# A two-block network on one core: half of twelve experts' last projection moved behind the experts, beside the first products of the next layer

## The chip, the cores and the metric

The kernel runs on 1 core of one Trainium2 chip. The metric is device time in microseconds. Its engines are called as in the profile: PE (TensorE's matmuls), PEld (its weight loads), DVE (VectorE), ACT (ScalarE), POOL (GpSimd) and SP (the queue that issues nearly all loads).

## The reference, cut to what matters

256 tokens of width 1024 pass through a first block (a mixer and 16 experts), a normalisation, and two layers of a second block. Everything is float32.

```python
# first block, after the mixer
h = rmsnorm(x, g_ffn[l])
aff = jax.nn.softmax((h @ w_router[l]).astype(f32), axis=-1)
vals, idx = lax.top_k(jnp.swapaxes(aff, 1, 2), cap)          # cap = 32 tokens an expert
xe = h[bidx, idx]
gt = jnp.einsum('becd,edf->becf', xe, w_gate[l])              # 1024 -> 2048
up = jnp.einsum('becd,edf->becf', xe, w_up[l])
ye = jnp.einsum('becf,efd->becd', jax.nn.silu(gt) * up, w_down[l])   # 2048 -> 1024
ye = ye * vals[..., None].astype(ye.dtype)
x = x + jnp.zeros_like(x).at[bidx, idx].add(ye.astype(dt))
return rmsnorm(x, g_final)
# second block, for l in 0, 1
x = x + 0.5 * swiglu(rms_norm(x, norm_ffn1[l]), ffn1_wi[l], ffn1_wo[l])   # wi: 1024 -> 2 * 2816
h = rms_norm(x, norm_mix[l]); p = h @ w_in[l]
...                                                            # recurrent mixer, chunk attention, pooling of p_c
x = x + jnp.concatenate([y_a, y_b, y_c], axis=-1) @ w_out[l]
x = x + memory_cross_attention(...)
x = x + 0.5 * swiglu(rms_norm(x, norm_ffn2[l]), ffn2_wi[l], ffn2_wo[l])
```

## The kernel before

The 256 tokens lie as two tiles of 128 (`t` = 0, 1) in `s.x`. The kernel is written once through, fully unrolled, and a scheduler turns the order of the text into an order for each engine; each engine, and the load queue SP, then works through its own list in order. A load waits there until its slot is free.

**The expert stage** (`moe`). For each of the 16 experts `e`, 16 slices of w_gate and w_up and 8 slices of w_down, 1 MiB each, are loaded in the order of their use by `wload` (lines 930 and 934). A slice is used by four products of 32 stationary columns (the expert's 32 tokens, or a quarter of the hidden channels), which stand beside each other in PE (lines 1020 and 1050; each is recorded as two matmuls, so a slice has eight). After the 16 slices a Silu, a product and four transposes give `ht`, the hidden activations with channels on partitions. The 8 slices of w_down give 512 output channels for each `b` of 0 and 1, four slices (`t`) for each. The result `ye` is scattered back to the tokens by a product with `sc`, a transposed one-hot matrix with the router's weights (line 1062), and added to `s.x` (line 1063). Tokens are fetched for the experts by the products in `gather` (line 1006): expert 0's own first, those of experts 1 to 15 behind all its products with w_down.

Where a slice lands is fixed by a list of 18 places and two spare ones that are used once. After the first 20 slices, the 18 take turns:

```python
SPARE = ["X", "K1"]
RING2 = ["hTh", "hTl", "L0", "L1", "decay", "U", "z", "hA", "R", *["ring"] * 4, "xa", *["spl"] * 3, "sd"]
```

Places are buffers that the mixer before no longer needs; "ring" is the ring of four 8-KiB buffers through which the other layers load all their weights, and "spl" are the three pairs of buffers for split weights. X and K1 later hold the tokens of experts 4 to 15.

**The feed-forward layers** (`ffn`). `turn` transposes `s.x` to `s.hT` (channels on partitions, eight blocks `k` of 128 channels, each as a high part `hTh` and a low part `hTl`; lines 370 to 374). The factor of the normalisation is not in `hT`; it is applied to the products, since it is one number per token. A weight piece of 1 MiB (512 input channels by 512 outputs) is loaded to the ring, and `wsplit` splits each half of it into a high part `wh` (ACT, line 307) and a low part `wl` (DVE, line 308). `lin_A_steps` multiplies: for each half piece 12 matmuls of 512 columns (three terms, two blocks, two token tiles; line 468). Two pieces make a group with all 1024 input channels; a group for the gate and one for the up projection are followed by `ev_gate`, `ev_up` and `finish` (lines 1091, 1095, and 1079 to 1083: eight transposes and a split of the hidden activations). Five such pairs and one group of a gate and up half make 22 pieces. In the first layer (`first=True`) two normalisations follow on each other, `g_final` between them, so a chain of squares, sums and powers on DVE, ACT and POOL (lines 1101 to 1111) has to end before the first group is evaluated; it is placed behind the first two half pieces. The output product `out(b)` adds to `s.x` (line 1129); `lead` puts the first half of the next layer's `turn` inside `out(1)`.

**Banks.** Products accumulate in a pool of six PSUM banks (`acc`); a group holds two, a half of w_down one, a scatter one. Transposes have two banks of their own.

Of the kernel before, what the change touches and what calls it, by code (L numbers as in the profile page):

```python
# [236 lines left out]
RING2 = ["hTh", "hTl", "L0", "L1", "decay", "U", "z", "hA", "R", *["ring"] * 4, "xa", *["spl"] * 3, "sd"]  # L237
NF = 3
# [4 lines left out]
class Net:  # L243
    def __init__(s, ctx, tc, A):
# [8 lines left out]
        s.t2 = pool("t2", 5)  # L253
        s.acc = pool("acc", 6, space=PSUM)
# [17 lines left out]
    def slot(s, i, name, shape, dt=F32, tag=None):  # L272
        return s.sl.tile(shape, dt, name=name, tag=tag or f"s{i}")
# [104 lines left out]
    def turn(s, g):  # L378

        s.hT = [s.late.tile([P, KT, T], F32R, name=n, tag=n) for n in ("hTh", "hTl")]  # L380
        for b in range(2):
            s.to_T(s.x, g, *s.hT, kps=(2 * b, 2 * b + 1))
            yield
# [29 lines left out]
    def pieces(s, ap):  # L413

        w = None if ap is None else s.wload(ap)
        for c in range(2):
            yield s.piece() if ap is None else s.wsplit(w[:, 1024 * c:1024 * c + 1024])

# [29 lines left out]
    def lin_A_steps(s, aps, xT, kts, evac, cols=512, in_turn=False):  # L448
# [12 lines left out]
        for p in halves():  # L461
# [3 lines left out]
            for ts, part in ([((t,), terms) for t in range(2)] if last else [((0, 1), [u]) for u in terms]):  # L465
                for w, x, i, kk in part:
                    for t in ts:
                        s.nc.tensor.matmul(pss[t], x[:, n + kk, t * P:t * P + P], w[:, kk, :],  # L468
# [9 lines left out]
    def lin_A(s, aps, xT, kts, evac, cols=512):  # L478
        run(s.lin_A_steps(aps, xT, kts, evac, cols))


    def first(s):
        with s.tc.tile_pool(name="phmix", bufs=1) as s.sl:
# [433 lines left out]
    def moe(s):  # L917
        nc, A = s.nc, s.A
        E, C = 16, 32
        loads = itertools.count()  # L920
        V, VS = s.V1

        def wload(ap):


            i, n = next(loads), len(RING2)
            where = RING2[i] if i < n else SPARE[i - n] if i < n + 2 else RING2[(i - n - 2) % n]
# [84 lines left out]
        gather(0, (0, 1), 0, 1)  # L1012
        for e in range(E):
# [16 lines left out]
            pp = s.trb([P, T])  # L1030
            for t in range(2):
                rep = s.tmp([P, 4, C])
                nc.gpsimd.tensor_copy(rep, wt[:, t, e, :].unsqueeze(1).to_broadcast([P, 4, C]))  # L1033
                nc.tensor.transpose(pp[:, t * P:(t + 1) * P], rep.rearrange("p j c -> p (j c)"), s.ident)
            sc = s.tmp([P, T])
            nc.scalar.copy(sc, pp)
# [6 lines left out]
            ht = s.tmp([P, 4, P])  # L1043
            nc.vector.tensor_copy(ht, ph)
            py = [s.bank([P, 512]), s.bank([P, 512])]
            for b in range(2):
                for t in range(4):
# [823 lines left out]
```

## Time and profile before

| | |
|---|---|
| time, median of 3 runs | 2604.05 us (2599.95 to 2615.35) |
| the profiled execution | 2604.3 us, with a span of 2602.2 us |
| PE busy | 2258.5 us (87% of the span) |
| DVE busy | 1155.5 us (44%) |
| ACT busy | 842.0 us (32%) |
| chain that ended last | PE 56%, DMA 32%, DVE 8% |
| HBM read | 661.92 MB, 255 GB/s over the span |

The page divides the span into stages that look different: the mixer until about 360 us, the experts until about 1285 us, the second block behind them. Shares of the span are means over all of these. "Waits" and "chain" name what released an instruction; a window gives busy time in a stretch, in the order PE, PEld, DVE, ACT, POOL, with the number of instructions in brackets.

### The profile page before, as it was taken

Reading aid. Unit: us, or ns where it says so; the run is one execution under the profiler, and the core shown is the slowest. Engines: PE = TensorE matmul, PEld = TensorE weight load, DVE = VectorE, ACT = ScalarE, POOL = GpSimd, SP = SyncE. Lnnn points to the kernel's source line nnn. Section 1 sums busy time; section 2 is a strip of 40 time slices with the busy share of each in tenths; the row PEclk is TensorE's granted clock in tenths of the full one; section 3 lists DMA queues with packets and bytes.
Section 4 is the critical chain, followed back from the end, with each engine's and each line's share of the span. In section 5 each row is a group of like instructions: output and inputs, shape, how many; then the busy total and the mean of one; then the engine's idle time right before and its main releaser. Section 6 shows DMA issues by size and latency. Waiting matters only on the chain.

```text
span 2602.2 us, 33476 instructions
## 1 busy us (share of the span) xinstructions
PE 2258.5 (87%) x13705; PEld 1504.9 (58%) x13705; DVE 1155.5 (44%) x1699; ACT 842.0 (32%) x1297; POOL 226.9 (9%) x252
## 2 busy tenths in 40 slices
PE   7999888766666777666799999999999999999999
PEld 6988864111111111111288887788888888778887
DVE  6886843000000000000265586555555558665554
ACT  5653320000000000000244545355444445545543
POOL 3321300000000000000000141100000005110000
PEclk9999989878778777788899999999999999999999
DMA  5344589999999999999955524245555543424553
GB/s 200 130 146 140 235 316 407 420 426 425 426 425 426 425 426 425 426 426 426 387 207 175 180 95 160 83 163 192 179 191 181 182 175 112 144 86 166 185 179 129
DMA packets 104633, 665.14 MB, mean 256 GB/s; under 512 B 11808, under 2 KB 12192, under 8 KB 34848
## 3 DMA queue, kind: packets, MB, share of 16 engines
q1 hardware_dynamic: 103328, 660.12, 64.9%
q8 instruction: 107, 1.75, 0.3%
q10 hardware_dynamic: 1008, 1.84, 0.2%
q0 software_dynamic: 144, 1.05, 0.1%
q14 instruction: 46, 0.38, 0.0%
HBM read 661.92 MB, written 1.05 MB: 255 GB/s over the span
## 4 chain that ended last, share of the span: by engine, by line
PE 56%; DMA 32%; DVE 8%; ACT 2%; issue 1%; POOL 1%; SPq 0%; DVEq 0%; ACTq 0%; POOLq 0%
PE lA L468 32%; DMA wc<-in_w_down_dram 12%; DMA wc<-in_w_up_dram 10%; DMA wc<-in_w_gate_dram 9%; PE acc L430 7%; PE lA L1679 4%; DVE wl L308 1%; PE acc L1020 1%; PE acc L1006 1%; PE trb L1079 1%; PE acc L1050 1%; DMA wc<-in_ffn_wi_dram 1%; PE acc L313 1%; ACT wh L307 1%; PE acc L1441 1%
## 5 line engine op out<-in xcount | busy, mean ns | idle before, releaser
L308 DVE TENSOR_TENSOR wl<-wc,wh 128x1024 fp32r<-128x1024 f32 (+1 forms) x447 | 548.2, 1230 | 381.1 <-ACT wh L307 370.8
L307 ACT CAST wh<-wc 128x1024 fp32r<-128x1024 f32 (+1 forms) x454 | 471.9, 1042 | 551.3 <-PE lA L468 398.2
L1020 PE MATMUL acc<-wc,xe 128*32 128x512 f32 x2048 | 376.4, 786 | 174.2 <-DMA wc<-in_w_up_dram 92.8
L1020 PEld LDWEIGHTS acc<-wc,xe 128*32 128x32 f32 x2048 | 53.2, 121 | 482.3 <-DMA wc<-in_w_up_dram 220.6
L1039 DVE TENSOR_TENSOR tmp<-tmp,acc 128x512 f32<-128x512 f32 x16 | 11.0, 686 | 522.5 <-PE acc L1020 522.5
L468 PE MATMUL lA<-wh,hTl 128*128 128x512 f32 (+1 forms) x864 | 236.4, 390 | 0.0
L468 PE MATMUL lA<-wh,hTh 128*128 128x512 f32 (+1 forms) x864 | 230.0, 387 | 3.3 <-ACT hTh L373 3.3
L468 PE MATMUL lA<-wl,hTh 128*128 128x512 f32 (+1 forms) x864 | 228.0, 385 | 3.0 <-DVE wl L308 3.0
L1050 PE MATMUL acc<-wc,tmp 128*32 128x512 f32 x1024 | 170.4, 738 | 63.9 <-DMA wc<-in_w_down_dram 50.2
L468 PEld LDWEIGHTS lA<-wl,hTh 128*128 128x128 f32 x864 | 162.1, 189 | 34.4 <-DVE wl L308 4.1
L468 PEld LDWEIGHTS lA<-wh,hTh 128*128 128x128 f32 x864 | 160.9, 188 | 35.4 <-ACT hTh L373 5.1
L468 PEld LDWEIGHTS lA<-wh,hTl 128*128 128x128 f32 x864 | 159.0, 189 | 26.5
L1038 ACT ACTIVATE tmp<-acc 128x512 f32<-128x512 f32 x16 | 9.6, 597 | 508.8 <-PE acc L1020 508.8
L1063 DVE TENSOR_TENSOR x<-x,acc 128x512 f32<-128x512 f32 x64 | 44.0, 687 | 255.0 <-PE acc L1062 255.0
L1050 PEld LDWEIGHTS acc<-wc,tmp 128*32 128x32 f32 x1024 | 29.6, 123 | 187.9 <-DMA wc<-in_w_down_dram 104.2
L1059 ACT COPY tmp<-acc 128x512 f32<-128x512 f32 x32 | 18.7, 585 | 317.5 <-PE acc L1050 317.5
L468 PE MATMUL lA<-wl,hidh 128*128 128x512 f32 x352 | 96.1, 391 | 0.0
L468 PE MATMUL lA<-wh,hidh 128*128 128x512 f32 x352 | 94.4, 390 | 0.0
L468 PE MATMUL lA<-wh,hidl 128*128 128x512 f32 x352 | 94.1, 389 | 0.0
L430 PE MATMUL acc<-hTh,wl 128*128 128x256 f32 x544 | 81.3, 291 | 10.7 <-DVE wl L308 10.4
L430 PE MATMUL acc<-hTh,wh 128*128 128x256 f32 x544 | 85.9, 297 | 1.5 <-ACT wh L307 1.0
L1033 POOL COPY tmp<-ohwt 128x128 f32<-128x128 f32 x32 | 9.3, 293 | 847.4 <-PE trb L1042 646.0
(447 smaller groups left out, 3060.8 us busy)
## 6 DMA issues: line engine op xcount, KB each, us to landing
wc<-in_w_up_dram SPq DMA_DIRECT2D x117, 1024.0 KB, 18.4
wc<-in_w_gate_dram SPq DMA_DIRECT2D x102, 1024.0 KB, 18.5
wc<-in_w_down_dram SPq DMA_DIRECT2D x102, 1024.0 KB, 17.2
wc<-in_ffn_wi_dram SPq DMA_DIRECT2D x88, 1024.0 KB, 4.7
wc<-in_ffn_wo_dram SPq DMA_DIRECT2D x40, 1024.0 KB, 4.7
wc<-in_w_in_dram SPq DMA_DIRECT2D x39, 1024.0 KB, 4.7
wc<-in_w_gate_dram SPq DMA_DIRECT2D x52, 512.0 KB, 13.5
wc<-in_w_down_dram SPq DMA_DIRECT2D x52, 512.0 KB, 15.9
```

The costliest lines, as they stand in the source:

```text
L307: s.nc.scalar.copy(h[:, :n], w)
L308: (eng or s.nc.vector).tensor_tensor(l[:, :n], w, h[:, :n].bitcast(F32), op=OP.subtract)
L313: mm(out, a[0], b[0], start=start, stop=False)
L430: s.nc.tensor.matmul(ps[:, c, :], w[:, k, :], x[:, k, :], start=i + k == 0, stop=i == len(terms) - 1 and k == KT - 1)
L468: s.nc.tensor.matmul(pss[t], x[:, n + kk, t * P:t * P + P], w[:, kk, :], start=n + kk + i == 0, stop=i == 2 and n + kk == kts - 1)
L1006: nc.tensor.matmul(ps[:, i, :], s.x[:, t, k * P:(k + 1) * P], oh[:, t, 4 * g + lo:4 * g + hi].rearrange("p e c -> p (e c)"), start=t == 0, ...
L1020: nc.tensor.matmul(ps[32 * j:32 * j + 32, :], xe[e // 4, k // 4][:, k % 4, es], c(j), start=k == 0, stop=k == KT - 1)
L1050: nc.tensor.matmul(py[b][32 * j:32 * j + 32, :], ht[:, t, 32 * j:32 * j + 32], c(j), start=t == 0, stop=t == 3)
L1063: nc.vector.tensor_tensor(s.x[:, t, cs], s.x[:, t, cs], ps, op=OP.add)
L1079: nc.tensor.transpose(ps[:, j, t * P:(t + 1) * P], hs[t][:, (a + j) * P:(a + j + 1) * P], s.ident)
L1441: nc.tensor.matmul(ps[sl, it, :], lhs[sl, it, :], rhs[sl, it, :], start=True, stop=True, tile_position=(32 * gi, 32 * gi))
L1679: s.nc.tensor.matmul(pss[t], x[:, n + kk, t * P:t * P + P], w_[:, kk, :], start=n + kk + i == 0, stop=i == 2 and n + kk == KT - 1)
```

## The change

Experts 0 to 3 keep their order. For the last 12 experts (`LATE`) the main loop does only the first half of w_down (`b = 0`) and keeps `ht` in three places that leave the rotation from the second pass on (`KEPT`; 15 places stay). Behind expert 15, `turn` transposes channels 0 to 511, which are final then. A second loop does the second halves (`b = 1`) of the 12 experts; between its slices, from the sixth on, every second slice is followed by one step (half a piece) of `ffn_part`, which multiplies the first layer's 11 weight pieces for input channels 0 to 511 and copies the sums to six places (`PART`). In that loop slices rotate over six places (`EARLY_RING`), four of them the ring, which the pieces use as well. `ffn` then multiplies only channels 512 to 1023 in that layer (`products`) and adds the kept sums on DVE (`total`). Expert 0's gathers are placed between its second-half slices. `in_turn=b == 1` lets, in the last half piece of `out(1)`, all of token tile 0's matmuls come before tile 1's, with tile 0's sum evaluated between them, in all feed-forward layers and in the cross attention. `split_ahead` splits the pooling product's weights (`w_in[5]`) before the exponentials of the mixer instead of at the product. The places hTh and hTl, and those of `PART`, move to pools of their own.

```diff
 RING2 = [...]
+EARLY_RING = ["ring", "ring", "X", "ring", "ring", "K1"]
+LATE = 12
+KEPT = ["z", "R", "sd"]
+PART = ["L0", "L1", "decay", "U", "hA", "xa"]
...
     def moe(s):
...
-        loads = itertools.count()
+        rota = [[w for w in RING2 if w not in KEPT]]
+
+        def turns():
+            yield from RING2 + SPARE
+            while True:
+                now = rota[0]
+                for w in now:
+                    yield w
+                    if rota[0] is not now:
+                        break
+        places = turns()
...
-            i, n = next(loads), len(RING2)
-            where = RING2[i] if i < n else SPARE[i - n] if i < n + 2 else RING2[(i - n - 2) % n]
+            where = next(places)
...
+        def down(e, b, ht, sc):
+
+            py = s.bank([P, 512])
+            for t in range(4):
+                c = wload(A["w_down"][e, t, b])
+                for j in range(4):
+                    nc.tensor.matmul(py[32 * j:32 * j + 32, :], ht[:, t, 32 * j:32 * j + 32], c(j),
+                                     start=t == 0, stop=t == 3)
+                yield
+            cs = slice(512 * b, 512 * b + 512)
+            ye = s.tmp([P, 512])
+            nc.scalar.copy(ye, py)
+            for t in range(2):
+                ps = s.bank([P, 512])
+                nc.tensor.matmul(ps, sc[:, t * P:(t + 1) * P], ye, start=True, stop=True)
+                nc.vector.tensor_tensor(s.x[:, t, cs], s.x[:, t, cs], ps, op=OP.add)
+            yield
...
             if e == 0:
-                for g in range(4):
-                    for kk in (0, 4):
-                        gather(g, range(kk, kk + 4), int(g == 0), 4)
...
+                both = [down(e, b, ht, sc) for b in range(2)]
+                for j in range(8):
+                    next(both[j // 4])
+                    if j == 3:
+                        for kk in (0, 4):
+                            gather(0, range(kk, kk + 4), 1, 4)
+                    elif j > 3:
+                        for g, kk in others[2 * (j - 4):2 * (j - 4) + 2]:
+                            gather(g, range(kk, kk + 4), 0, 4)
+                for steps in both:
+                    run(steps)
+            else:
+                for b in range(2 if i < 0 else 1):
+                    run(down(e, b, ht, sc))
+
+
+        rota[0] = EARLY_RING
+        turn = s.turn(lambda k: s.gfg[:, k:k + 1])
+        next(turn)
+        parts = s.ffn_part()
+        n = 0
+        for e in kept:
+            steps = down(e, 1, kept[e], scale(e))
+            for _ in range(4):
+                next(steps)
+                n += 1
+                if n > 4 and n % 2 == 0 and n < 4 * LATE:
+                    next(parts, None)
+            run(steps)
+        run(parts)
+        run(turn)
+
+
+    def ffn_part(s):
+
+        wi = s.A["ffn1_wi"][0]
+        s.parts = {}
+        for i in range(6):
...
+            for g in range(2 if i < 5 else 1):
+                yield from s.lin_A_steps([wi[4 * i + 2 * g]], s.hT, 4,
+                                         lambda t, ps: s.nc.scalar.copy(s.parts[i][:, g, t, :], ps))
...
+            def products(c, evac):
+                if first:
+                    return s.lin_A_steps([wi[c + 1]], hT, 4, evac, k0=4)
+                return s.lin_A_steps([wi[c], wi[c + 1]], hT, 8, evac)
...
+                def total(j, t, ps, to=None):
+                    if not first:
+                        return ps
+                    to = s.tmp([P, 512]) if to is None else to
+                    nc.vector.tensor_tensor(to, ps, s.parts[i][:, j, t, :], op=OP.add)
+                    return to
...
-                    nc.scalar.activation(g[t], ps, AF.Silu, scale=r[:, t:t + 1])
+                    nc.scalar.activation(g[t], total(0, t, ps, g[t]), AF.Silu, scale=r[:, t:t + 1])
...
                     hs[t] = g[t]
+                    ps = total(1, t, ps)
...
-                return s.lin_A_steps([wo[5 * b + i] for i in range(5)] + [wt[b]], hid, 22, evac)
+                return s.lin_A_steps([wo[5 * b + i] for i in range(5)] + [wt[b]], hid, 22, evac, in_turn=b == 1)
...
+        w5 = s.split_ahead(w_in[5])
         nc.scalar.activation(flat(e1), flat(cl), AF.Exp)
...
-        s.lin_T(w_in[5], hT, lambda ps: vec.tensor_tensor(u, ps, rsb2, op=OP.mult))
+        s.lin_T(w5, hT, lambda ps: vec.tensor_tensor(u, ps, rsb2, op=OP.mult))
...
-        run(s.turn(lambda k: s.gfg[:, k:k + 1]))
```

## Rows read from the trace of the kernel before

**Rows 1.** The first line of the profile page

```profile
span 2602.2 us, 33476 instructions
```

**Rows 2.** Windows: us, busy us of each engine, granted clock, DMA, GB/s

```profile
452.00:1262.00 810.00, 563.62 (x2836) 100.59 (x2832) 56.39 (x82) 28.32 (x56) 7.93 (x27) 0.79 1.01 425
...
1298.00:1417.00 119.00, 119.00 (x545) 98.37 (x546) 70.19 (x79) 58.04 (x71) 2.53 (x3) 1.00 0.55 194
```

**Rows 3.** DMA issues: instruction and count, KB of each, median us to landing

```profile
wc<-in_w_down_dram SPq DMA_DIRECT2D x102, 1024.0 KB, 17.2
wc<-in_ffn_wi_dram SPq DMA_DIRECT2D x88, 1024.0 KB, 4.7
```

**Rows 4.** Timeline of the expert stage: start us, us, engine, line, operation, idle before

```profile
430.94 11.37 PE L1020 MATMUL acc<-wc,xe 128*32 128x512 f32 x104
...
442.23 0.44 PE L1034 MATMUL trb<-ident,tmp 128*128 128x128 f32 x2
...
1190.75 1.93 PE L1020 MATMUL acc<-wc,xe 128*32 128x512 f32 x8 [1.35 <-DMA wc<-in_w_gate_dram]
...
1275.51 1.98 PE L1062 MATMUL acc<-tmp 128*128 128x512 f32 x4
```

**Rows 5.** Chain of waits in the first feed-forward layer: start us, us, what

```profile
1312.80 0.22 PE trb L1079 x2
...
1314.14 21.33 PE lA L468 x94
1335.47 0.22 PE trb L1079 x2
```

**Rows 6.** Timeline at the end of the expert stage

```profile
1281.80 1.06 PE L1050 MATMUL acc<-wc,tmp 128*32 128x512 f32 x8 [1.15 <-DMA wc<-in_w_down_dram]
1282.93 0.58 ACT L1059 COPY tmp<-acc 128x512 f32<-128x512 f32 x1 [9.16 <-PE acc L1050]
...
1283.57 1.98 PE L1062 MATMUL acc<-tmp 128*128 128x512 f32 x4 [0.71 <-ACT tmp L1059]
...
1285.59 0.69 DVE L1063 TENSOR_TENSOR x<-x,acc 128x512 f32<-128x512 f32 x1 [0.17 <-PE acc L1062]
...
1297.95 1.21 PE L468 MATMUL lA<-wl,hTh 128*128 128x512 f32 x4 [1.36 <-DVE wl L308]
```

**Rows 7.** Windows behind the first expert, and at the first feed-forward loads

```profile
431.00:433.00 2.00, 2.00 (x21) 0.61 (x24) 0.69 (x1) 0.00 (x0) 0.00 (x0) 1.00 0.13 49
433.00:435.00 2.00, 2.00 (x24) 0.65 (x20) 0.00 (x0) 0.00 (x0) 0.00 (x0) 1.00 0.96 303
...
1285.00:1290.00 5.00, 3.74 (x18) 2.28 (x17) 4.83 (x8) 3.69 (x8) 0.00 (x0) 1.00 1.01 423
```

**Rows 8.** Timeline of the first expert: gathers, and the load queue beside them

```profile
413.01 14.56 PE L1006 MATMUL acc<-ohwt,x 128*128 128x96 f32 x128
...
415.27 21.41 SPq L930 DMA_DIRECT2D wc<-in_w_down_dram  x8
```

**Rows 9.** Windows of 10 us in the expert stage

```profile
450.00:460.00 10.00, 9.61 (x62) 2.85 (x58) 2.38 (x4) 1.45 (x3) 0.29 (x1) 1.00 1.00 403
...
470.00:480.00 10.00, 6.22 (x32) 0.77 (x32) 0.00 (x0) 0.00 (x0) 0.00 (x0) 0.66 1.01 425
```

**Rows 10.** Groups by line, 1335 to 1381 us: busy, mean ns, idle before

```profile
L308 DVE TENSOR_TENSOR wl<-wc,wh 128x1024 fp32r<-128x1024 f32 x16 | 19.6, 1224 | 16.4 <-ACT wh L307 16.2
...
L1095 DVE SCALAR_TENSOR_TENSOR tmp<-lA,rs,tmp 128x512 f32<-128x512 f32 x6 | 4.2, 747 | 3.3 <-PE lA L468 3.3
```

**Rows 11.** Groups by line, 1205 to 1262 us

```profile
L1063 DVE TENSOR_TENSOR x<-x,acc 128x512 f32<-128x512 f32 x4 | 2.7, 686 | 18.0 <-PE acc L1062 18.0
```

**Rows 12.** Waits of PE behind 1300 us: in total, times, longest

```profile
PE acc L430 <- DVE wl L308: 5.5, 1, 5.5
...
PE trb L1193 <- POOL rs L359: 2.2, 2, 1.1
```

**Rows 13.** The chain's last additions

```profile
2597.11 0.69 DVE x L1129
```

More of the change, by code (lines that the diff above doesn't have):

```diff
@@ L272, in slot @@
     def slot(s, i, name, shape, dt=F32, tag=None):
-        return s.sl.tile(shape, dt, name=name, tag=tag or f"s{i}")
+        pool = s.late if i in ("hTh", "hTl") else s.part if i in PART else s.sl
+        return pool.tile(shape, dt, name=name, tag=tag or f"s{i}")
     def tmp(s, shape, dt=F32):
@@ L378, in turn @@
     def turn(s, g):
-        s.hT = [s.late.tile([P, KT, T], F32R, name=n, tag=n) for n in ("hTh", "hTl")]
+        if not s.padded:
+            s.padded = s.late.tile([P, 120], F32, name="spare")
+        s.hT = [s.slot(n, n, [P, KT, T], F32R) for n in ("hTh", "hTl")]
         for b in range(2):
@@ L476, in lin_A_steps, with lin_A @@
             yield
-    def lin_A(s, aps, xT, kts, evac, cols=512):
-        run(s.lin_A_steps(aps, xT, kts, evac, cols))
+    def lin_A(s, aps, xT, kts, evac, cols=512, k0=0):
+        run(s.lin_A_steps(aps, xT, kts, evac, cols, k0=k0))
     def first(s):
+        s.late = s.ctx.enter_context(s.tc.tile_pool(name="late", bufs=1, side="right"))
+        s.part_pool = ExitStack()
+        s.part = s.part_pool.enter_context(s.tc.tile_pool(name="part", bufs=1, side="right"))
         with s.tc.tile_pool(name="phmix", bufs=1) as s.sl:
@@ L1029, in moe @@
                         onehot(wt, lambda t: aff[:, t, i:i + 1], i)
[L1030 to L1036, printed above, removed]
+            sc = scale(e)
             h = s.tmp([P, 512])
@@ L1052, in moe @@
-            if e == 0:
-                for g in range(4):
-                    for kk in (0, 4):
-                        gather(g, range(kk, kk + 4), int(g == 0), 4)
-            for b in range(2):
-                cs = slice(512 * b, 512 * b + 512)
-                ye = s.tmp([P, 512])
-                nc.scalar.copy(ye, py[b])
-                for t in range(2):
-                    ps = s.bank([P, 512])
-                    nc.tensor.matmul(ps, sc[:, t * P:(t + 1) * P], ye, start=True, stop=True)
-                    nc.vector.tensor_tensor(s.x[:, t, cs], s.x[:, t, cs], ps, op=OP.add)
+            i = e - (E - LATE)
@@ L1112, in ffn @@
                 run(gate)
-                s.lin_A([wi[4 * i + 2], wi[4 * i + 3]], hT, 8, ev_up)
+                run(products(4 * i + 2, ev_up))
                 if first and i == 2:
@@ L1120, in ev_last @@
                 hs[t] = s.tmp([P, 256])
+                if first:
+                    both = s.tmp([P, 512])
+                    nc.vector.tensor_tensor(both, ps, s.parts[5][:, 0, t, :], op=OP.add)
+                    ps = both
                 nc.scalar.activation(hs[t], ps[:, 0:256], AF.Silu, scale=r[:, t:t + 1])
@@ L1123, in ev_last @@
                                                op1=OP.mult)
[L1124 removed]
+            run(products(20, ev_last))
             finish(20, 2, hs)
@@ L1365, in mix_ @@
         s.mem_parts(l)
-        yh, yl = [s.late.tile([P, KT, T], F32R, name=n, tag=n) for n in ("hTh", "hTl")]
+        yh, yl = [s.slot(n, n, [P, KT, T], F32R) for n in ("hTh", "hTl")]
         ps = s.bank([P, 2, T])
```

52 lines of the change are left out of this document (36 added, 16 removed).

## The prediction

> **What bounds the kernel now.** I read the busy shares by stage first, then the chain of waits, then the timeline at the seams. Three regimes have to be seen. In the expert stage the weights arrive at 425 GB/s with every DMA engine busy and TensorE busy for 563.6 of 810 us at a mean granted clock of 0.79; in the first feed-forward layer behind it TensorE is busy 119 of 119 us at clock 1.00, while DMA runs at 194 GB/s [rows 2]. So the expert stage is set by bytes and the next one by matmuls, and each leaves the other's resource idle. One load of 1 MiB costs 1.049 MB / 425 GB/s = 2.47 us of the first stage. The third thing is the seam: the last slice of w_down begins its matmuls at 1281.80, and the feed-forward products then still have transposes, casts and a normalisation chain in front of them [rows 6].
>
> The products run in a fixed rhythm. Four 1-MiB pieces and their eight transposes take 1335.47 - 1312.80 = 22.67 us, and 94 of these matmuls take 21.33 us, 0.227 us each [rows 5]; a piece has 24, so 5.45 us. Twenty-two pieces make 5.5 groups or 124.7 us. Counting back one group from 1312.80 gives an effective start at 1290.1, 8.3 us behind the last slice [rows 5, 6], and an end at 1414.8.
>
> **The products that move (gain).** Eleven of the twenty-two pieces (contraction rows 0 to 511) are multiplied beside the late second halves of w_down. The feed-forward layer loses 11 x 5.45 = **-59.9 us**.
>
> **Their loads (loss).** The eleven loads move too, into the stage where bytes set the time, past nothing that could hide them: 11 x 2.47 = **+27.1 us**. The w_down slices themselves only change their place in the queue, so their bytes cost nothing more.
>
> **Whether TensorE keeps up there.** Thirteen slices of four 32-column products took 11.37 us without a wait, 0.87 us each; the scatter of one half takes 1.98 us and the two transposes of the scale 0.44 us [rows 4]. One late expert with a piece beside it is 4 x 0.87 + 1.98 + 0.44 + 5.45 = 11.35 us of TensorE against 5 x 2.47 = 12.3 us of loads: 92% busy, still set by bytes. The slack is only 1 us per expert, and the order of TensorE is fixed: a product half waits there for its ScalarE and VectorE split, and the slices behind it wait with it. The ring shrinks to six slots (four of them shared with the moved pieces), so some 4 to 5 loads can be outstanding where a w_down load now takes 17.2 us to land and a feed-forward load 4.7 us [rows 3]. Four slots did hold 423 GB/s for the first feed-forward loads [rows 7], and 4.7 us is two loads of transfer, so I do not expect starvation; stalls of half a microsecond per expert to two are the bounds, 0 to +20 us in all with the start and end of the stage. I take **+6 us**, near the full-rate row.
>
> **Fewer slots in the first expert.** Three of the 18 slots in rotation are reserved from the first pass on. The place where slots are short is visible: while gathers occupy TensorE for 14.56 us, the queue issues the next loads only as slots come free, and the rate falls to 49 and 303 GB/s in four microseconds [rows 7, 8]. With three loads fewer allowed ahead, the gap grows by 3 x 2.47 = 7.4 us. The diff also puts the gathers between the second half's slices; this frees those slots later, not sooner, since each slice now stands behind two gathers (128 of these matmul records in 14.56 us, so 3.6 us for two gathers). The bounds are 0 (slots come free in time after all) and +10; I take **+7.4 us**.
>
> **The seam.** Before, a slice, a copy, the scatter and the addition followed on 1281.80 (additions done at 1285.59 + 0.69 = 1286.28) and a split stalled TensorE once more at 1297.95 [rows 6]. After, only channels 512 to 1023 remain to be transposed and one last half product can fill the wait. I count 8.1 us from the last slice to the next product, 8.3 before: **-0.2 us**, bounds -3 and +3.
>
> **What is left of the feed-forward layer.** Each half-length product now ends in a bank that VectorE must add to the kept part. For a gate and an up group VectorE has four splits of 1.22, four additions (0.69, as the residual addition from PSUM), two multiplications of 0.75 and two hidden remainders (taken at 0.69 too): 4.9 + 2.8 + 1.5 + 1.4 = 10.6 us [rows 10, 11], against 10.9 + 0.9 = 11.8 us of TensorE. It fits, at 90%, where the whole layer had 59% [rows 2]. Behind the first group stands the normalisation chain, ready some 12 us after the first product; TensorE has three groups' banks (16 us) until it must wait for it. I take **+3 us**, bounds 0 and +8. The copies of the parts out of PSUM are 22 ScalarE copies in the expert stage, where ScalarE is nearly idle; with that cover gone they would be about 0.6 us each.
>
> **The small edits.** The only stall at the pooling product is one wait of 5.5 us for a split, in one layer [rows 12]. Splitting earlier moves the split ahead of long VectorE work, whose total stays the same and which the next group's splits also stand behind: **-2.5 us**, between -5.5 and +2. At layers' ends TensorE is kept busy by the next stage's first half, except for two waits on the reciprocal root, 2.2 us in sum [rows 12]; token tiles in turn hide the first tile's addition (0.69, as the last one of the kernel [rows 13]). In the cross attention's ends the same edit finds no wait to remove. **-1.5 us** over all, between -4 and 0. The new pool layout issues nothing and costs nothing.
>
> **Sum.** -59.9 + 27.1 + 6 + 7.4 - 0.2 + 3 - 2.5 - 1.5 = **-20.6 us**. The profiled execution has a span of 2602.2 [rows 1] and its own time is 2604.3, within 0.3 us of the median 2604.05. The forecast is 2604.3 - 20.6, rounded to **2584 us**.
>
> **Rivals.**
>
> *The clock stays low beside the loads (the other side).* In 470 to 480 us TensorE, busy 62%, had clock 0.66; in 450 to 460, busy 96%, it had 1.00 [rows 9]; over the expert stage 70% busy went with 0.79 [rows 2]. A slice takes 1.93 us at the lower level [rows 4]. If the late stage gets mean clock c, a late expert needs 11.35/c: from c = 0.92 down it passes the loads. At 0.79 eleven experts lose 11 x (14.4 - 12.3) = 23 us, which leaves about 2600; at 0.66 they lose 54 us and the kernel ends near 2631. Without the 6 us of stalls, which this replaces, it is slower by 13 us from c = 0.71 down. Against it: 92% busy lies near the rows with 1.00, and once TensorE falls behind it never idles. Chance of a slower result by this: 0.09.
> The Trainium skill, in "TensorE: Matmul & The Clock Gate", section "HAM oscillation — how this bites in real kernels", says that a loop whose burst of matmuls is shorter than its wait for the next load falls back to the lower clock in every round. The expert stage's 0.79 agrees with it; by that rule the late stage is safe only as long as its bursts outlast its waits, which 11.35 of 12.3 us allows.
>
> *VectorE becomes the bound behind the experts.* If additions at a group's end hold up the next splits by 1.4 us in each of eleven groups, 15 us instead of 3: about 2596. For it: 90% against 59%; against it: three split buffers run ahead. Chance 0.13.
>
> *The small ring starves the queue.* If two slots at a time wait behind a product, a tenth of the rate over 59 loads (145.7 us) is lost: 15 us instead of 6, or 2593; a quarter lost is 49 us, or 2627. Chance 0.15, mostly the mild form, 0.03 for the other.
>
> *The gain is larger.* No slots are missed at the first expert, the late stage keeps the full rate, and the pooling wait goes entirely: -20.6 - 7.4 - 6 - 3 = -37 us, 2567. Chance 0.13.
>
> *It doesn't do what it says:* the products wait until the last slice and only the loads move. Then the 59.9 us come back: slower by far. TensorE's order is as written unless loads land out of turn, which one queue does not allow; 0.01.
>
> **How the numbers follow.** The likeliest case has the remaining 0.49 and spans 2574 to 2593. A change within 0.5% (13 us, 2591 to 2617) is about what a measurement of this kernel cannot tell from none. Faster: 0.45 of the likeliest, 0.13 larger gain, 0.08 from the mild forms of the VectorE and ring rivals: 0.66. Slower: 0.09 + 0.03 + 0.01, 0.13 in all. Same: 0.21. For eight in ten I leave one in ten out on either side: 2565 to 2608.
>
> **What would show it.** Full rate through to the last w_down slice, some 35 to 42 us later than 1281.80, with clock above 0.92 in the last 145 us before it, supports the main terms; a rate under 400 GB/s there means the ring, a clock below 0.9 with TensorE fully busy means the clock. The gap at 431 us should widen to about 10 us. The rest of the feed-forward products should take about 65 us behind the seam; more, with waits on VectorE, is the VectorE rival. The wait of 5.5 us should be mostly gone. The forecast is wrong above all if the late stage is not set by bytes.

## The result: 26 us less, where 21 were forecast

The changed kernel took 2579.26 us (median of four runs, 2576.03 to 2583.82) beside 2605.39 for the kernel before (2599.95 to 2615.35): 26.1 us less, a ratio of 0.9897 (95% interval 0.9862 to 0.9931; ratios below have theirs in brackets). Its profiled execution took 2577.74 us, 26.6 less than that of before. Forecast were 2584 and -20.6.

The first line of the page, and then windows of the changed kernel (us, busy us of PE, PEld, DVE, ACT and POOL with their records, granted clock, DMA share, GB/s): the plain expert stage, the late stage in which pieces and w_down halves alternate, and the remaining products.

```profile
span 2576.0 us, 33572 instructions
```
```profile
452.00:1160.00 708.00, 494.94 (x2448) 85.81 (x2444) 41.33 (x60) 22.16 (x45) 7.83 (x29) 0.78 1.01 425
1200.00:1300.00 100.00, 96.44 (x504) 48.33 (x496) 29.90 (x32) 32.30 (x49) 4.23 (x16) 1.00 1.01 421
1340.00:1394.00 54.00, 54.00 (x258) 44.24 (x257) 48.36 (x66) 31.99 (x43) 1.70 (x3) 1.00 0.54 195
```

Against [rows 2] there is a third kind of stage now: from 1200 to 1300 both DMA (421 GB/s) and TensorE (96% busy, clock 1.00) are full. Behind it, VectorE is busy 48.36 of 54 us, 90%; the forecast's count for a gate and an up group was 90%.

Two places split the difference. The seam, as a timeline of TensorE (start us, us, engine, line, operation, records, idle before), and the last product of channels 512 to 1023:

```profile
1319.03 1.06 PE L1058 MATMUL acc<-wc,kept 128*32 128x512 f32 x8
...
1326.13 1.18 PE L483 MATMUL lA<-wh,hTh 128*128 128x512 f32 x4 [1.53 <-ACT wh L313]
...
1334.07 1.20 PE L483 MATMUL lA<-wl,hTh 128*128 128x512 f32 x4 [1.68 <-DVE wl L314]
...
1336.78 0.50 PE L483 MATMUL lA<-wh,hTh 128*128 128x512 f32 x1 [0.82 <-ACT wh L313]
...
1393.54 1.07 PE L483 MATMUL lA<-wl,hTh 128*128 128x512 f32 x4
```

The same last product in the kernel before:

```profile
1413.28 1.07 PE L468 MATMUL lA<-wl,hTh 128*128 128x512 f32 x4
```

A w_down load lands after 12.3 us in the middle now, where it was 17.2 [rows 3] (the DMA issues of the page):

```profile
wc<-in_w_down_dram SPq DMA_DIRECT2D x110, 1024.0 KB, 12.3
```

The last w_down slice comes at 1319.03 instead of 1281.80 [rows 6], 37.2 us later. From it to the last product it is 74.51 us instead of 131.48, 57.0 us shorter. So the changed kernel is 19.7 us ahead at the end of these products, and 26.2 at the end of the span. The first group of matmuls behind the slice now waits three times, for splits.

The 5.5 us wait of the pooling product and the two waits on the reciprocal root [rows 12] are gone. The largest of TensorE's waits between 1420 and 2200 us that is left (total, times, longest):

```profile
PE lA L483 <- DVE wl L314: 4.3, 3, 2.7
```

In the kernel before this group had one wait of 0.8. So about half of the pooling product's wait did not vanish: it comes back as one of 2.7 us, for another split, at the next products (at 1506.89 us).

### The profile page after: what moved, and what is told of

Read it like the earlier page. It is cut to its first block, busy times and chain, and to the rows that moved or that the text cites. A ratio compares the mean times of both kernels' runs of the same rounds, so it can differ in the third digit from the quotient of the medians.

```text
span 2576.0 us, 33572 instructions
## 1 busy us (share of the span) xinstructions
PE 2263.1 (88%) x13729; PEld 1505.2 (58%) x13729; DVE 1170.3 (45%) x1721; ACT 857.3 (33%) x1331; POOL 233.6 (9%) x276
## 4 chain that ended last, share of the span: by engine, by line
PE 55%; DMA 32%; DVE 9%; ACT 2%; issue 2%; POOL 1%; SPq 0%; ACTq 0%; DVEq 0%; POOLq 0%
PE lA L483 31%; DMA wc<-in_w_up_dram 15%; DMA wc<-in_w_gate_dram 10%; PE acc L445 7%; DMA wc<-in_ffn_wi_dram 3%; PE lA L1785 3%; DMA wc<-in_w_down_dram 3%; DVE wl L314 2%; PE acc L1058 1%; ACT wh L313 1%; PE acc L1080 1%; PE trb L1167 1%; PE acc L1034 1%; PE acc L319 1%; PE acc L321 1%
## 5 line engine op out<-in xcount | busy, mean ns | idle before, releaser
L1080 PE MATMUL acc<-wc,xe 128*32 128x512 f32 x2048 | 385.4, 777 | 169.7 <-DMA wc<-in_w_up_dram 85.8
L1058 PE MATMUL acc<-wc,kept 128*32 128x512 f32 x768 | 122.1, 751 | 14.2 <-DVE kept L1104 9.4
L1046 POOL COPY tmp<-ohwt 128x128 f32<-128x128 f32 x56 | 15.2, 293 | 919.6 <-PE acc L1066 627.5
L445 PE MATMUL acc<-hTl,wh 128*128 128x256 f32 x544 | 82.0, 290 | 2.3 <-DVE hTl L380 2.3
L445 PE MATMUL acc<-hTh,wl 128*128 128x256 f32 x544 | 78.1, 286 | 4.9 <-DVE wl L314 4.9
## 6 DMA issues: line engine op xcount, KB each, us to landing
wc<-in_w_down_dram SPq DMA_DIRECT2D x110, 1024.0 KB, 12.3
wc<-in_w_up_dram SPq DMA_DIRECT2D x102, 1024.0 KB, 17.2
wc<-in_w_up_dram SPq DMA_DIRECT2D x52, 512.0 KB, 14.8
```

Of the source, the lines that this page charges most:

```text
L445: s.nc.tensor.matmul(ps[:, c, :], w[:, k, :], x[:, k, :], start=i + k == 0, stop=i == len(terms) - 1 and k == KT - 1)
L1058: nc.tensor.matmul(py[32 * j:32 * j + 32, :], ht[:, t, 32 * j:32 * j + 32], c(j), start=t == 0, stop=t == 3)
L1080: nc.tensor.matmul(ps[32 * j:32 * j + 32, :], xe[e // 4, k // 4][:, k % 4, es], c(j), start=k == 0, stop=k == KT - 1)
```

## Experiments

For the terms ahead of the seam one number serves all runs: the time from the first gather's first matmul to the last w_down matmul of the stage. Behind it another does: the time from there to the first transposes of the last group of the feed-forward layer. Both are starts of named instructions in the traces, in us:

```
kernel                     first gather   last w_down   between   then to the last group
before                        369.40        1282.27      912.87        134.1
changed                       370.33        1319.51      949.18         77.3
changed, run again            369.01        1318.25      949.24         77.3
changed, third run            369.72        1319.05      949.33         77.3
18 slots                      372.17        1312.66      940.49         77.3
18 slots, run again           370.57        1311.68      941.11         77.4
gathers behind both halves    369.22        1317.05      947.83         77.3
one load                      368.43        1321.78      953.35         76.0
no products                   370.64        1316.61      945.97         78.9
first piece split early       370.36        1311.34      940.98         78.1
no additions                  371.62        1320.73      949.11         77.1
18 slots, VectorE alone       370.37        1311.81      941.44         75.3
no split ahead                369.22        1317.97      948.75         77.3
token tiles not in turn       369.53        1321.20      951.67         77.3
```

In executions of the same kernel the last column repeats to 0.1 us and the one before it to 0.2 (the changed kernel, three times) and 0.6 (18 slots, twice). The whole time does not: see the run of the same kernel again.

### The gap in the first expert: slots or the order of the gathers?

The rate behind the first expert, in the kernel before and in the changed one (windows, columns as above):

```profile
404.00:431.00 27.00, 27.00 (x204) 17.93 (x207) 7.32 (x11) 1.17 (x2) 0.29 (x1) 0.92 1.01 421
431.00:452.00 21.00, 19.27 (x175) 5.71 (x174) 2.06 (x3) 1.44 (x3) 0.29 (x1) 1.00 0.91 373
```
```profile
404.00:431.00 27.00, 27.00 (x204) 17.64 (x199) 8.01 (x12) 1.17 (x2) 0.29 (x1) 0.96 0.81 311
431.00:452.00 21.00, 19.27 (x162) 5.56 (x154) 1.38 (x2) 0.97 (x2) 0.29 (x1) 0.92 0.94 387
```

110 GB/s less over 27 us and 14 more over 21 us are 2.68 MB, 6.3 us at 425 GB/s. Two kernels take the two causes apart. **All 18 slots until the third expert:**

```diff
-        rota = [[w for w in RING2 if w not in KEPT]]
+        rota = [RING2]
 ...
+            if e == 2:
+                rota[0] = [w for w in RING2 if w not in KEPT]
```

> The changed kernel, but the three reserved places stay in the rotation until expert 2 and leave it then. Slot theory: the gap behind the first expert (rates of 311 and 387 GB/s in 404 to 431 and 431 to 452 us, 9.1 us of loads lost, against 2.8 us before the change) comes from the three missing slots; with 18 slots again the loss falls back to about 3 to 4 us, and the last w_down slice comes 5 to 6.5 us earlier than 1319.0, the whole kernel 5 to 6.5 us below the changed one's 2577.7, near 2572. Rival, order theory: the gap comes from the gathers that now stand between the second half's slices; then nothing moves by more than 1 us.

The gap closes (windows of this kernel when it was run again):

```profile
404.00:431.00 27.00, 27.00 (x200) 17.60 (x193) 7.33 (x11) 1.17 (x2) 0.29 (x1) 0.94 1.01 424
431.00:452.00 21.00, 19.27 (x159) 5.66 (x162) 2.07 (x3) 0.97 (x2) 0.29 (x1) 0.92 0.96 389
```

From first gather to last w_down it takes 940.5 and 941.1 us against 949.2: 8.1 to 8.7 us come back. The first execution took 2576.08 us in all, since it reached the gathers 1.8 us later than the changed kernel's and, against that execution, lost 1.5 us at 1459 to 1470 and 3.0 us at 2250 to 2312 us. Slot theory, then: the time between the marks came back whole, and more of it than the expected 5 to 6.5 us; the whole time of that one execution did not show it.

**The gathers behind both halves, 15 slots:** the gathers of the next experts are issued behind the second half of the first expert instead of between its slices.

> The changed kernel with expert 0's gathers behind both halves of w_down again, in the order of before, and 15 slots. Slot theory: slot 16 of the sixteenth-last slice is not free until expert 1 starts, whatever the order, so the same 6 us stay lost, the rate in 404 to 452 us is the same in sum, and the kernel is within 1.5 us of the changed one. Order theory: the gap closes to that of before and the kernel gains about 6 us, near 2571.

The gap stays:

```profile
404.00:431.00 27.00, 27.00 (x220) 18.18 (x216) 8.01 (x12) 1.17 (x2) 0.30 (x1) 0.98 0.75 306
431.00:452.00 21.00, 18.51 (x154) 5.54 (x150) 2.75 (x4) 1.56 (x3) 0.59 (x2) 1.00 1.01 417
```

2580.09 us in a single execution; 947.8 between the two marks, 1.4 less than in the changed kernel (the second window has 417 GB/s instead of 387). So the slots are the cause, and the order adds about a sixth of it.

### What sets the pace of the late stage?

**One load:** ten of the eleven piece loads are left out, and all piece products use the one that was loaded. It stays in one of the six rotating places, so the slices have five.

> All eleven products of the late stage use one loaded piece, so ten of the eleven moved loads are left out (and one of six rotating places); the later layer's sums are those of other weights. If bytes set the late stage with TensorE close behind, as I hold: an expert with a product, 12.46 us now, falls only to TensorE's 11.35, and the last slice comes 11 to 13 us earlier than 1319.0. If TensorE has room, it falls by the whole 24.7 us. If TensorE already sets the pace, nothing moves.

**No products:** the pieces are loaded and split, but not multiplied.

> The eleven pieces are loaded and split in the late stage, but their matmuls are left out and the kept sums are zeros. If bytes set the late stage: the last slice comes at most 3 us earlier than 1319.0, and 59.9 us of matmuls in it are shown to be free. If TensorE's order sets the pace, or the products hold up the slots: 5 us or more earlier. The feed-forward layer behind it keeps its length.

Windows of the late stage, first with one load, then without the products:

```profile
1200.00:1240.00 40.00, 38.88 (x199) 18.22 (x192) 11.48 (x12) 12.96 (x19) 1.76 (x6) 1.00 0.92 341
1240.00:1280.00 40.00, 38.82 (x194) 18.56 (x193) 12.47 (x13) 12.07 (x18) 1.76 (x6) 1.00 0.88 324
```
```profile
1200.00:1240.00 40.00, 26.10 (x130) 6.16 (x122) 13.55 (x14) 10.50 (x14) 1.78 (x6) 0.83 1.01 423
1240.00:1280.00 40.00, 24.91 (x126) 5.51 (x122) 11.23 (x13) 8.65 (x12) 1.77 (x6) 0.83 1.01 427
```

With ten loads less, 25 us of DMA time at 2.47 each, the stretch is 4.2 us longer, not 11 to 13 shorter: that expectation fell, and TensorE sets the pace of this kernel. It stays 97% busy there and waits for no load, and its scatters come every 12.84 us (two lines of that kernel's timeline). Most of the 4.2 us are ten waits of 0.39 us on the copy ahead of the scatter, 3.9 us in sum; in the changed kernel part of a piece's product stands in that place, and there is one such wait.

```profile
1233.26 1.98 PE L1066 MATMUL acc<-tmp 128*128 128x512 f32 x4 [0.39 <-ACT tmp L1063]
...
1246.10 1.98 PE L1066 MATMUL acc<-tmp 128*128 128x512 f32 x4 [0.39 <-ACT tmp L1063]
```

Without the products the stretch is 3.2 us shorter, at the full rate, and the last slice comes 2.9 us earlier: within the 3 us that the expectation allowed if bytes set the pace. So the products beside the slices cost 3.2 us, and the late stage has two limits within half a microsecond of each other per expert. One late expert of the changed kernel, as TensorE's timeline:

```profile
1235.51 0.38 PE L1047 MATMUL trb<-ident,tmp 128*128 128x128 f32 x2
1235.82 1.92 PE L1058 MATMUL acc<-wc,kept 128*32 128x512 f32 x16
1238.30 1.21 PE L483 MATMUL lA<-wh,hTh 128*128 128x512 f32 x4 [0.55 <-ACT wh L313]
1239.34 1.09 PE L483 MATMUL lA<-wh,hTl 128*128 128x512 f32 x4
1240.27 1.08 PE L483 MATMUL lA<-wl,hTh 128*128 128x512 f32 x4
1241.28 1.06 PE L1058 MATMUL acc<-wc,kept 128*32 128x512 f32 x8
1242.28 1.20 PE L483 MATMUL lA<-wh,hTh 128*128 128x512 f32 x4
1243.31 1.08 PE L483 MATMUL lA<-wh,hTl 128*128 128x512 f32 x4
1244.32 1.06 PE L1058 MATMUL acc<-wc,kept 128*32 128x512 f32 x8
1245.32 1.20 PE L483 MATMUL lA<-wl,hTh 128*128 128x512 f32 x4
1246.35 1.88 PE L1066 MATMUL acc<-tmp 128*128 128x512 f32 x4
1248.07 0.38 PE L1047 MATMUL trb<-ident,tmp 128*128 128x128 f32 x2
```

From 1235.51 to 1248.07 it is 12.56 us with a wait of 0.55: 12.0 us of matmuls, not 11.35, against 12.34 us of loads. Waits like that one, for a split, come to 7.0 us in eleven from 1180 to 1320 us, while the loads kept 421 GB/s from 1200 to 1300. The slices alone take 1.0 us each where they stand between products (0.87 in a row [rows 4]), and the piece takes 6.05 us in three parts (2.98, 2.04 and 1.03) instead of 5.45.

The clock: at 96% busy the late stage has 1.00; without the products, at 62 to 65%, it has 0.83. There the slices of 1.06 us stand behind waits for loads that are longer, and the clock falls to the lower of its two levels between these two lines of the timeline without products (the second slice takes 1.93 us):

```profile
1214.40 1.06 PE L1058 MATMUL acc<-wc,kept 128*32 128x512 f32 x8 [3.79 <-DMA wc<-in_w_down_dram]
1216.85 1.93 PE L1058 MATMUL acc<-wc,kept 128*32 128x512 f32 x8 [1.38 <-DMA wc<-in_w_down_dram]
```

The Trainium skill, "TensorE: Matmul & The Clock Gate", section "HAM oscillation — how this bites in real kernels", says that bursts shorter than the waits for loads fall back to the lower clock each round. The trace agrees in part: the clock falls, but not in each round, since the slices at 1202.17 and 1204.59 us, behind waits of 1.68 and 1.35, still took 1.06. In the kernel before it is the same: three slices of 1.06 us behind waits of 1.4 come before the one of 1.93 in [rows 4], and the 0.79 that the prediction cites is the mean of stretches at both levels.

### The seam: additions, the early split, or GpSimd?

**The kept sums are not added:**

```diff
-                    if not first:
-                        return ps
+                    return ps
 ...
-                if first:
+                if False:
```

> The changed kernel without the additions of the kept sums (it leaves them out, so the sums over channels 0 to 511 are lost in the first feed-forward layer). Theory A, the additions on VectorE are what the first group behind the seam waits for: the stretch from the last w_down slice to the end of the products, 80.9 us in the changed kernel, becomes 77 to 78.5 us. Theory B, the seam's waits are those for the splits of the first pieces and the normalisation chain, whatever is added: within 1 us of 80.9. Both: no difference per pair of groups (11.8 us) once the products run.

77.1 us to the last group against 77.3; the 1.0 to 1.4 us that the groups between are ahead (34.1 instead of 35.5 at the second) are given back by the last. (The 80.9 us of the expectation were counted to the end of the last transposes, 1399.90; TensorE no longer waits for those.) The additions are not what the seam costs: theory B. 2582.57 us in all.

**18 slots, and the first remaining piece split early** (shown against the kernel with 18 slots):

```diff
         rota = [RING2]
 ...
+        s.early0 = s.split_ahead(s.A["ffn1_wi"][0][1])
 ...
-                    return s.lin_A_steps([wi[c + 1]], hT, 4, evac, k0=4)
+                    return s.lin_A_steps([s.early0 if c == 0 else wi[c + 1]], hT, 4, evac, k0=4)
```

> The changed kernel with all 18 slots in rotation until the third expert (the three that hold pieces leave it only then), and with the first of the remaining pieces of the gate weights loaded and split before the products' turn comes. Theory of the slots: the rate between 404 and 431 us is back at about 424 GB/s, and the experts start and end 6 to 8 us sooner than in the changed kernel. Theory of the seam (part of the 5 us lost there is the split of the first remaining piece): another 1.5 to 2.5 us, so the products start some 11 to 12 us behind the last slice instead of 13.5. Together 8 to 10 us below the changed kernel beside it, near 2570. Rival, the early split takes VectorE or ScalarE from the expert stage or its load delays a slice: the slots' 6 to 8 us alone, or less. Rival, what is gained is lost later, as part of it was in the single run with 18 slots: 3 to 5 us.

2571.09 us (2570.75 to 2575.82), a ratio of 0.9864 [0.9847, 0.9881] to the kernel before. But the seam gained nothing: the first of its waits is shorter, the other two are gone, and a new one stands behind them in TensorE's timeline of this kernel, for the first group's gated product:

```profile
1318.58 1.20 PE L486 MATMUL lA<-wh,hTh 128*128 128x512 f32 x4 [1.18 <-ACT wh L313]
...
1334.80 0.66 PE L1173 MATMUL trb<-ident,tmp 128*128 128x128 f32 x2 [2.44 <-DVE tmp L1201]
```

To the last group it takes 78.1 us, 0.8 more. The 18 slots alone, timed:

> The changed kernel with all 18 slots in rotation until the third expert, and nothing else, timed. In the run of the same kernel before, the experts came 8.2 us sooner than in the changed kernel, counted from the start of the gathers. Theory, the early split in the faster version added nothing (its stretch behind the last slice was no shorter): 2569 to 2573 us, the same as that version within 1.5 us. Rival, the early split did save 1.5 us or more: 2573 to 2575 us.

2571.87 us (2571.41 to 2572.88), 0.9875 [0.9859, 0.9892]: the same within 0.8 us, as the theory had it.

**What is slow there is VectorE beside GpSimd.** The two engines in the changed kernel, 10 us behind the last slice:

```profile
1329.26 1.78 DVE L1207 TENSOR_TENSOR x<-x,gf 128x512 f32<-128x512 f32 x1
1330.97 1.24 DVE L357 TENSOR_TENSOR sst<-ss 128x2 f32<-128x2 f32 x1
1332.13 0.68 DVE L1207 TENSOR_TENSOR x<-x,gf 128x512 f32<-128x512 f32 x1
```
```profile
1328.83 3.37 POOL L1207 TENSOR_TENSOR x<-x,gf 128x512 f32<-128x512 f32 x2 [7.29 <-DVE tmp L353]
```

The same multiplication takes 1.78 us on VectorE while GpSimd multiplies, and 0.68 a little later. The kernel before has the same sharing, and its VectorE is stretched too, though less: 1.22 and 0.74 us for operations that take 0.68 and 0.15 elsewhere in both traces.

```profile
1291.43 1.22 DVE L347 SCALAR_TENSOR_TENSOR tmp<-x 128x512 bf16<-128x512 f32 x1
...
1293.38 0.74 DVE L351 TENSOR_TENSOR sst<-ss 128x2 f32<-128x2 f32 x1
```

The kernel with 18 slots and all four multiplications on VectorE:

```diff
-  (nc.gpsimd if t else nc.vector).tensor_tensor(xv, xv, s.gf[:, 512 * b:512 * b + 512], op=OP.mult)
+  nc.vector.tensor_tensor(xv, xv, s.gf[:, 512 * b:512 * b + 512], op=OP.mult)
```

> The version with 18 slots, with the four multiplications by the norm's weight behind the experts all on VectorE instead of two of them on GpSimd. In that version the transposes of the first, second and last group behind the seam start 24.6, 35.6 and 77.4 us after the last w_down slice. Theory A, VectorE's operations there (1.78 and 1.24 us where others of the kind take 0.68 and 0.15) were stretched by GpSimd beside them: now four of about 0.68 us, the reciprocal root sooner, and 77.4 becomes 76 to 77. Theory B, the multiplications only move to the engine that is short of time there: the first group comes up to 1 us later, the last one at 77.4 or up to 1 us later. Theory C, the long operations are not GpSimd's doing: they keep their 1.78 and 1.24 us. Time: 2571 to 2573 us in all cases, so the trace decides.

```profile
1321.56 0.69 DVE L1209 TENSOR_TENSOR x<-x,gf 128x512 f32<-128x512 f32 x1
1322.17 0.15 DVE L357 TENSOR_TENSOR sst<-ss 128x2 f32<-128x2 f32 x1
1322.24 0.69 DVE L1209 TENSOR_TENSOR x<-x,gf 128x512 f32<-128x512 f32 x1
1322.84 0.16 DVE L363 TENSOR_SCALAR ms<-sst 128x2 f32<-128x2 f32 x1
1322.91 1.28 DVE L1209 TENSOR_TENSOR x<-x,gf 128x512 f32<-128x512 f32 x2
```

Four multiplications take 2.66 us here, two beside GpSimd took 2.46; the chain behind them (the 128 x 2 addition) starts 0.6 us after the first one instead of 1.7; and the stretch is shorter by 2.1 us (75.3 against 77.4), more than theory A's 0.4 to 1.4. The Trainium skill, "SBUF — State Buffer", says that a VectorE instruction with two SBUF inputs contends with a GpSimd instruction that reads SBUF (section "Who interferes with whom"), and that whichever of the two starts first keeps the shared ports for its whole instruction while the other is blocked (section "SBUF: two separate sides"). The rows agree: of VectorE's 1.78 and 1.24 us, 0.68 and 0.15 are the work, and the second ends at 1332.21, with GpSimd's second multiplication at 1332.20. The reciprocal root of the second normalisation is ready 13.2 us after the first remaining product here, 14.8 with 18 slots and GpSimd. In all, 2568.39 us (2563.51 to 2575.89), 0.9867 [0.9847, 0.9887], the fastest median of the study, though its ratio is no lower than the 0.9864 of the early split; the 2.1 us are shown by the trace, while its runs spread over 12 us and the time alone does not separate it from the 18 slots.

### The small edits, and how far two executions differ

**The changed kernel again**, beside the next two:

> The changed kernel once more, as the measure for the three that run beside it and for how far two executions differ. Both theories of the tail: about 2579 us, 24 to 27 us below the kernel before. If the step of about 3.7 us that other executions show between 2250 and 2312 us (layer 1's mixer) appears here too, it is no matter of an edit but of the execution, and differences of that size at the end of a single trace say nothing.

2577.38 us (2572.49 to 2579.82), 0.9881 [0.9863, 0.9900], 28.7 below the kernel before beside it. A third, single run of the same text (meant to have the four multiplications on VectorE, which its text does not) took 2580.42. The step at 2250 to 2312 us is there: against the changed kernel's first execution the run again loses 4.0 us in it, and the third run 3.1. The instructions are the same; the clock is not (PE busy, clock, DMA, GB/s; first execution, then the run again):

```profile
2250.00:2312.00 62.00, 56.50 (x681) 0.97 0.26 86
```
```profile
2250.00:2312.00 62.00, 56.49 (x616) 0.89 0.24 82
```

So it belongs to the execution, and the profiled execution of the changed kernel was the lucky one of the three. **Without the split ahead:**

```diff
-        w5 = s.split_ahead(w_in[5])
 ...
-        s.lin_T(w5, hT, lambda ps: vec.tensor_tensor(u, ps, rsb2, op=OP.mult))
+        s.lin_T(w_in[5], hT, lambda ps: vec.tensor_tensor(u, ps, rsb2, op=OP.mult))
```

> The changed kernel with the pooling weight's split back in its old place. Theory of the forecast (the split ahead gains 2 to 3 us): the 5.5 us wait of the pooling product in layer 0 is back, and the time is 2 to 3 us above the changed kernel's beside it, since about half of the wait was given back at the next products. Rival, the whole wait is gained: 5 us or more above. Rival, all of it is given back behind the next group: no difference over 1 us at the end of the layer, although the wait is back.

2582.66 us (2579.26 to 2585.47). The wait is back:

```profile
PE acc L445 <- DVE wl L314: 5.4, 1, 5.4
```

Beside the run again, this kernel is 0.3 us ahead at 1489 us, before that product, 1.3 behind at 1512, 0.9 at 1580 and 0.7 at 1687. So the edit gains 1.0 to 1.2 us of its 5.4 in layer 0 by the trace, less than the 2 to 3 expected: with the split ahead, the wait of 2.7 us stands at the products behind. In layer 1, where the old place costs no such wait, nothing is gained that can be read: a split's wait at 2181 us is 1.3 us with the edit and 0.8 without, the lag goes from 0.7 to 0.3 there and is 0.9 at 2236. The medians differ by 5.3 us with spreads of 6 and 7 us; which part of that belongs to the edit stays open.

**Without the token tiles in turn.** This kernel also undoes the same order in the output product of the first block's mixer, which the kernel before already had; so its time is no pure measure of the edit, and only the junctions are read.

```diff
-            return s.lin_A_steps(None, mm, 8, evac, in_turn=b == 1)
+            return s.lin_A_steps(None, mm, 8, evac)
 ...
-                ... [wt[b]], hid, 22, evac, in_turn=b == 1)
+                ... [wt[b]], hid, 22, evac)
 ...
-                return s.lin_A_steps([wo[2 * b], wo[2 * b + 1]], oT, 8, evac, in_turn=b == 1)
+                return s.lin_A_steps([wo[2 * b], wo[2 * b + 1]], oT, 8, evac)
```

> The changed kernel without the token tiles in turn (first feed-forward layers and cross attention). Theory of the forecast (each junction at a layer's end gains one hidden addition, 0.7 us): 1 to 2 us above the changed kernel's beside it. Rival, TensorE has the next stage's first half to do there anyway: within 0.7 us of it, and its milestones around 1430 to 1460 us agree within 0.5 us.

2581.89 us (2579.06 to 2586.29). The two waits on the reciprocal root are back:

```profile
PE trb L1298 <- POOL rs L365: 2.2, 2, 1.1
```

Yet across the junction of layer 0 this kernel's lag behind the changed one (run again) goes from 2.96 to 2.61 us, and is 2.77 at 1480; in layer 1 it goes from 3.28 to 2.93, and is 3.09 at 2136. The edit gains nothing there, it costs some 0.2 to 0.35 us at each: TensorE had the first group's products to do. At the kernel's last addition, behind which nothing follows, it gains: the lag grows from 3.25 to 3.62 us. Most of the lag is older than these junctions. It arises in the first gathers, where the clock differs; windows of 372 to 380 us (PE, PEld, DVE, ACT and POOL, clock, DMA, GB/s; the first one has PE alone) in the kernel before, the changed one again, and this one:

```profile
372.00:380.00 8.00, 8.00 (x40) 0.50 0.67 231
```
```profile
372.00:380.00 8.00, 8.00 (x64) 3.27 (x56) 0.23 (x1) 0.00 (x0) 0.00 (x0) 0.88 0.67 232
```
```profile
372.00:380.00 8.00, 8.00 (x40) 2.97 (x36) 0.23 (x1) 0.00 (x0) 0.00 (x0) 0.50 0.63 221
```

Without a gap TensorE gets 0.50 of the clock in two of these executions and 0.88 in the third. Counted from the first gather, the lower level ends after 11.2 and 11.5 us in this kernel and the kernel before, and after 4.8 to 6.3 in all twelve other traces, the changed kernel's three among them (4.9 to 5.0). Two executions of one kernel differ by 1.0 us here (18 slots, 4.9 and 5.9). Whether the late rise belongs to these two kernels or to their executions, no run shows; each has one trace.

## Why the prediction was right

**Products, seam and the rest of the layer: right.** Forecast were -59.9 - 0.2 + 3 = -57.1 us; measured are -57.0 from the last slice to the last product. The +3 was taken for VectorE being 90% busy. VectorE is 90% busy, but the additions do not cost it (0.2 us less without them); the loss lies in the first group, where GpSimd holds up VectorE's normalisation chain (2.1 us back without GpSimd). So the size was right and the mechanism only near: the prediction had the chain "ready some 12 us after the first product" and no contention in it; in the changed kernel it is ready after 14.8 us. That the sum came out to 0.1 us is partly luck.

**Loads, late stage, slots: 40.5 forecast, 36.3 measured** (949.18 - 912.87). The slots took 8.1 us by experiment (7.4 forecast), and their cause was the one named. With 27.1 for the loads' bytes that leaves 1.1 us for stalls, where +6 was taken; or 3.5 us, if the kernel before is given the same clock in the first gathers (with 0.50 in place of 0.88 there the kernel without token tiles in turn has 2.4 us more between the two marks). The kernel without the products speaks for the second figure: it took 3.2 us off the stage. This term was mis-sized within its bounds. Its reason needs a correction as well: TensorE's slack was not 1 us per expert but 0.3, since where slices and products take turns the matmuls take 12.0 us instead of 11.35. The stage is not "set by bytes" alone but by both: 25 us less of loads did not shorten it, and 59.9 us less of products shortened it by 3.2.

**Pooling split and token tiles: -4.0 forecast.** Behind the last product, the profiled execution gained 6.4 us, the run again 3.2 (24.2 at the end of the span against 21.0). The step of 4.0 us at 2250 to 2312 us, the clock's, is more than that difference. By the traces the split gave 1.0 to 1.2 us in layer 0 and nothing to be read in layer 1, and the token tiles gave 0.4 at the kernel's end and cost about as much at the junctions; so these two terms were too large, and some 2 us of the run again are not traced to an edit.

The sum: 36.3 - 57.0 + 0.9 (the gathers began later) - 6.4 = -26.2 us of span, against -20.6; for the run again it is 36.4 - 57.0 - 0.4 - 3.2 = -24.2. The surplus of 5.6 us is 4.2 from the stage ahead of the seam and 2.4 behind it, less the 0.9. The part behind the seam is the clock of that one execution, since the run again does not have it; 2.4 us of the part ahead go with the low clock in the first gathers of the kernel before, in its one trace.

**The rivals.** The clock stayed at 1.00 all through the late stage. The queue did not starve (421 GB/s). VectorE did not become the bound: from the third group's transposes to the fifth's it is 23.7 us (46.9 and 70.6 behind the slice), 11.8 a pair, as counted. The larger gain of 2567 us needed the slots, and with them back it is nearly what came out, 2568 to 2572.

## What to carry to other kernels

Work moved from a stage with a full engine into one with a full queue gains the difference of the two prices (here 5.45 us of products against 2.47 us of load per piece), until both are full; take the price of each matmul from a stretch in which both kinds alternate, because the difference uses up the slack of the receiving stage (here 12.0 us instead of 11.35). Buffers reserved for a later stage should stay in rotation until that stage is near: three of 18 slots held back from the start cost 8 us, about a third of the whole gain, and holding them back from the third expert on cost none of that. Before an elementwise step is shared between VectorE and GpSimd, look at the durations on both: half the work took VectorE 2.46 us beside GpSimd, and the whole of it 2.66 alone.

## What the runs showed of the hardware

VectorE's two-input operations were stretched beside GpSimd's: 0.68 to 1.78 us for 128 x 512, and 0.15 to 1.24 us for 128 x 2; alone, four of 128 x 512 took 2.66 us. GpSimd's own went from 1.28 us each in the kernel before to 3.37 for two. And the granted clock over the same instructions differed between executions of one kernel (0.97 and 0.89 at 2250 to 2312 us), which moves a whole execution by 3 to 4 us: in this kernel no single trace tells an edit of that size from chance by its end, while the time between two named instructions behind the experts repeats to 0.1 us.
